# Batched matrix product on one core: x loaded four batches at a time, in place of one batch at a time

## The chip, the cores and the metric

The kernel runs on one core of a Trainium2 chip. The metric is the device time in microseconds (us). A core has five engines that matter here: PE (TensorE, matrix products and transposes), DVE (VectorE) and ACT (ScalarE), which copy and cast, POOL (GpSimd), and SP (SyncE), which only issues transfers. Transfers between HBM (the chip's main memory) and SBUF (the core's working memory, 128 partitions) are carried by 16 DMA engines. PE writes its results to PSUM, from which DVE or ACT copy them to SBUF.

## What is computed

```python
batch, dim_i, dim_j, dim_k = 32, 256, 512, 384
x: (32, 256, 512) float32      y: (32, 512, 384) float32

def reference(x, y):
    return np.einsum('bij,bjk->bik', x, y).astype(np.float32)
```

Each of 32 batches is a product of a 256x512 with a 512x384 matrix. A batch's x is 512 KB, its y 768 KB and its result 384 KB. All of it is read or written once: 16.8 MB, 25.2 MB and 12.6 MB.

## The kernel before

P is 128, NI = 2 (256 rows of i over 128 partitions) and NJ = 4 (512 values of j over 128 partitions). PE contracts over partitions, so x must stand with j on the partitions. HBM has it with i on them, so each batch of x is transposed on PE first.

Five steps are done for each batch b, each by a function of its own:

- `load(b)` (L56) issues two transfers on SP's queue. L61 brings x[b] with two neighbouring rows to each partition: one run of 4 KB per partition. L62 brings y[b] with four neighbouring rows to each partition: one run of 6 KB.
- `transpose(b)` (L64) makes eight 128x128 float32 transposes on PE (L70), two to a PSUM tile of 128x256. DVE (L72) and ACT (L74) copy two such tiles each to `xt_sb` and cast them to float16. The columns of j are taken with a stride of four (`t::NJ`), which fits the four rows of y that stand on one partition.
- `round_y(b)` (L76) casts y[b] to float16 in four pieces of 128x384, two on ACT (L81) and two on DVE (L83).
- `multiply(b)` (L85) makes eight float16 products of 128x128 with 128x384 (L94), which add up in two PSUM tiles.
- `collect(b)` (L103) copies these to `o_sb`, one on ACT (L109) and one on DVE (L111). `store(b)` (L114) issues the result's transfer (L123), one run of 3 KB per partition. It stands on SP's queue, except for batches 27, 29 and 31 (`ON_ACT`), which ACT issues.

The order is written out by hand: `keep` holds every engine to the program's order. Five batches are loaded ahead (`AHEAD`), and then step s of the main loop does `load(s+5)`, `collect(s-2)`, `transpose(s)`, `round_y(s)`, `multiply(s-1)`, `store(s-2)`. In step 31 alone the product of batch 30 stands ahead of the transposes.

Two further things set the order of transfers. SP works its issues off in order, so a store that waits for its results holds up the loads behind it. And the framework gives the transfers eight completion semaphores in turn, so that each issue also waits until the transfer eight places before it has landed. In the program's order of SP, for instance, the 18th issue (a load of x) waits for the semaphore that the 10th used. So at most eight transfers are in flight.

Buffers: seven of x and seven of y, four each of `y_r` and `xt_sb`, eight of `o_sb`, and four PSUM tiles each for the transposes and for the products.

Of the kernel before, what the change touches and what calls it, by code (L numbers as in the profile page):

```python
# [1 line left out]

# [5 lines left out]


MM_DT = mybir.dt.float16  # L10
F32 = mybir.dt.float32
P = 128
AHEAD = 5

ON_ACT = (27, 29, 31)
GROUPS = [1, 1, 1, 1, 1, 1, 1, 1, 1, 1, 1, 1, 1, 1, 1, 1, 1, 1, 1, 1, 1, 1, 1, 1, 1, 1, 1, 1, 1, 1, 1, 1]

@with_exitstack  # L20
def kernel(
    ctx: ExitStack,
    tc: tile.TileContext,
    x: bass.AP,
    y: bass.AP,
    out: bass.AP,
):
    nc = tc.nc

    B, I, J = x.shape  # L30
    _, _, K = y.shape

    NI = I // P
    NJ = J // P

    const_pool = ctx.enter_context(tc.tile_pool(name="const", bufs=1))
    x_pool = ctx.enter_context(tc.tile_pool(name="x_pool", bufs=AHEAD + 2))
    y_pool = ctx.enter_context(tc.tile_pool(name="y_pool", bufs=AHEAD + 2))
    yr_pool = ctx.enter_context(tc.tile_pool(name="yr_pool", bufs=4))
    xt_pool = ctx.enter_context(tc.tile_pool(name="xt_pool", bufs=4))  # L40
    o_pool = ctx.enter_context(tc.tile_pool(name="o_pool", bufs=8))
    tpsum_pool = ctx.enter_context(tc.tile_pool(name="tpsum", bufs=4, space=bass.MemoryType.PSUM))
    opsum_pool = ctx.enter_context(tc.tile_pool(name="opsum", bufs=4, space=bass.MemoryType.PSUM))


    keep = tc.keep_in_program_order

    identity = const_pool.tile([P, P], F32)
    make_identity(nc, identity)


    place = [(g, i, n) for g, n in enumerate(GROUPS) for i in range(n)]
    assert len(place) == B
    x_of, y_of, yr_of, xt_of, ps_of, o_of = {}, {}, {}, {}, {}, {}

    def load(b):  # L56


        x_of[b] = x_pool.tile([P, NI, J], F32, name="x_sb")
        y_of[b] = y_pool.tile([P, NJ, K], F32, name="y_sb")  # L60
        keep(nc.sync.dma_start(out=x_of[b], in_=x[b].rearrange("(p r) j -> p r j", p=P)))  # L61
        keep(nc.sync.dma_start(out=y_of[b], in_=y[b].rearrange("(q t) k -> q t k", q=P)))  # L62

    def transpose(b):  # L64
        x_sb = x_of.pop(b)
        xt_of[b] = xt_pool.tile([P, NJ, NI, P], MM_DT, name="xt_sb")
        for t in range(NJ):
            t_ps = tpsum_pool.tile([P, NI, P], F32, name="t_ps")
            for r in range(NI):
                keep(nc.tensor.transpose(t_ps[:, r], x_sb[:, r, t::NJ], identity))  # L70
            if t % 2 == 0:
                keep(nc.vector.tensor_copy(xt_of[b][:, t], t_ps))  # L72
            else:
                keep(nc.scalar.copy(xt_of[b][:, t], t_ps))  # L74

    def round_y(b):  # L76
        y_sb = y_of.pop(b)
        yr_of[b] = yr_pool.tile([P, NJ, K], MM_DT, name="y_r")
        for t in range(NJ):
            if t % 2 == 0:  # L80
                keep(nc.scalar.copy(yr_of[b][:, t], y_sb[:, t]))  # L81
            else:
                keep(nc.vector.tensor_copy(yr_of[b][:, t], y_sb[:, t]))  # L83

    def multiply(b):  # L85
        xt_sb, y_r = xt_of.pop(b), yr_of.pop(b)
        ps_of[b] = [
            opsum_pool.tile([P, K], F32, name=f"o_ps_{r}", tag="o_ps")
            for r in range(NI)
        ]  # L90
        for t in range(NJ):
            for r in range(NI):
                keep(
                    nc.tensor.matmul(  # L94
                        ps_of[b][r],
                        xt_sb[:, t, r],
                        y_r[:, t],
                        start=(t == 0),
                        stop=(t == NJ - 1),
                    )  # L100
                )

    def collect(b):  # L103
        g, i, n = place[b]
        if i == 0:
            o_of[g] = o_pool.tile([P, n, NI, K], F32, name="o_sb", tag=f"o_sb_{min(n, 2)}")
        for r in range(NI):
            if r % 2 == 0:
                keep(nc.scalar.copy(o_of[g][:, i, r], ps_of[b][r]))  # L109
            else:  # L110
                keep(nc.vector.tensor_copy(o_of[g][:, i, r], ps_of[b][r]))  # L111
        del ps_of[b]

    def store(b):  # L114
        g, i, n = place[b]
        if i < n - 1:
            return
        o_sb = o_of.pop(g)
        dst = out[b - i : b + 1].rearrange("b (p r) k -> p b (r k)", p=P)
        src = o_sb.rearrange("p b r k -> p b (r k)")  # L120
        if n == 1:
            eng = nc.scalar if b in ON_ACT else nc.sync
            keep(eng.dma_start(out=dst[:, 0], in_=src[:, 0]))  # L123

    for b in range(AHEAD):
        load(b)
    for s in range(B + 2):
        if s + AHEAD < B:
            load(s + AHEAD)
        if s >= 2:  # L130
            collect(s - 2)
        if s == B - 1:
            multiply(s - 1)
        if s < B:
            transpose(s)
            round_y(s)
        if 1 <= s != B - 1 and s <= B:
            multiply(s - 1)
        if s >= 2:
            store(s - 2)  # L140


# [1 line left out]
_INS = ['x', 'y']  # L144
_OUTS = [((32, 256, 384), 'float32')]


# [23 lines left out]
```

## Time and profile before

| | |
|---|---|
| device time, median of 3 runs | 137.59 us (137.29 to 137.73) |
| device time of the profiled execution | 137.29 us |
| span of that execution, first to last instruction | 135.5 us |
| granted TensorE clock | 0.993 of full |
| bytes moved | 54.64 MB, 403 GB/s over the span |
| packets (one per run, and one per transfer and DMA engine for its semaphore) | 13833, of them 1536 under 512 B |
| busy: PE, DVE, ACT | 82.2, 64.5 and 66.7 us (61, 48 and 49%) |
| x, y and result: median us from issue to landing (on SP's queue) | 10.2, 11.2, 10.9 |

[...] Busy shares are of the span. "DMA" in the profile is the mean busy share of the 16 DMA engines, and "GB/s" what they moved. The busy share can read a little above 1, because an engine's packets overlap. A mean busy time of one PE instruction includes its overlap with its neighbours.

### The profile page before, as it was taken

To read this page: it belongs to the slowest core of one execution; us is meant where nothing else is said; L and a number is where in the kernel's file an instruction comes from. 1 tells how busy PE (TensorE), PEld (TensorE's weight loads), DVE (VectorE), ACT (ScalarE), POOL (GpSimd) and SP (SyncE) were. 2 spreads that over 40 slices of the span, in tenths; PEclk is the share of its full clock that TensorE was granted. 3 is DMA by queue.
4 is the path that set the end of the run, shared out by engine and by line. 5 is a ranking of instruction groups with operands and counts; after the bars stand their busy time and mean duration, and the time that the engine had idled before them with its cause. 6 is when DMAs were issued, how large, how long until landed. Compare 5 with 4: busy or idle time off the path is not lost.

```text
span 135.5 us, 1734 instructions
## 1 busy us (share of the span) xinstructions
PE 82.2 (61%) x512; PEld 57.4 (42%) x512; DVE 64.5 (48%) x160; ACT 66.7 (49%) x161; POOL 0.7 (1%) x6
## 2 busy tenths in 40 slices
PE   0579778857256775555775555775555775559340
PEld 0466555535233554333554333554333554335310
DVE  0445766656146644546644546644545644545430
ACT  3257766666056644446644446644446644446430
POOL 2000000000000000000000000000000000000000
PEclk9999999999999999999999999999999999999997
DMA  4999999999999999999999999999999999999993
GB/s 154 408 423 420 416 416 416 391 418 418 412 419 412 427 417 420 420 416 418 428 420 418 414 423 421 424 420 418 415 424 420 410 425 421 415 418 419 412 393 130
DMA packets 13833, 54.64 MB, mean 403 GB/s; under 512 B 1536, under 2 KB 1536, under 8 KB 13824
## 3 DMA queue, kind: packets, MB, share of 16 engines
q1 hardware_dynamic: 13392, 53.35, 96.5%
q10 hardware_dynamic: 432, 1.18, 2.2%
q8 instruction: 4, 0.07, 0.2%
q14 instruction: 5, 0.04, 0.1%
HBM read 41.94 MB, written 12.58 MB: 402 GB/s over the span
## 4 chain that ended last, share of the span: by engine, by line
DMA 89%; SPq 2%; PE 2%; issue 1%; DVE 1%; ACT 1%; ACTq 0%
DMA y_sb<-in_y_dram 34%; DMA x_sb<-in_x_dram 30%; DMA out_dram<-o_sb 25%; PE o_ps L94 1%; SPq L61 1%; SPq L62 1%; PE t_ps L70 1%; DVE o_sb L111 1%; ACT y_r L81 0%; ACT o_sb L109 0%; ACTq L123 0%; SPq L123 0%
## 5 line engine op out<-in xcount | busy, mean ns | idle before, releaser
L70 PE MATMUL t_ps<-identity,x_sb 128*128 128x128 f32 x256 | 39.9, 301 | 46.8 <-DMA x_sb<-in_x_dram 44.0
L70 PEld LDWEIGHTS t_ps<-identity,x_sb 128*128 128x128 f32 x256 | 34.4, 211 | 57.6 <-DVE o_sb L111 44.1
L74 ACT CAST xt_sb<-t_ps 128x256 f16<-128x256 f32 x64 | 23.8, 373 | 55.5 <-issue 39.5
L72 DVE CAST xt_sb<-t_ps 128x256 f16<-128x256 f32 x64 | 27.1, 425 | 49.2 <-PE t_ps L70 47.3
L94 PE MATMUL o_ps<-y_r,xt_sb 128*128 128x384 f16 x256 | 47.4, 330 | 1.1 <-ACT y_r L81 1.1
L81 ACT CAST y_r<-y_sb 128x384 f16<-128x384 f32 x64 | 29.6, 510 | 6.2 <-DMA y_sb<-in_y_dram 5.8
L94 PEld LDWEIGHTS <-xt_sb 128*128 128x128 f16 x256 | 25.7, 100 | 14.6 <-issue 1.8
L83 DVE CAST y_r<-y_sb 128x384 f16<-128x384 f32 x64 | 20.1, 356 | 12.4 <-DMA y_sb<-in_y_dram 12.1
L111 DVE COPY o_sb<-o_ps 128x384 f32<-128x384 f32 x32 | 17.8, 558 | 4.6 <-PE o_ps L94 2.1
L109 ACT COPY o_sb<-o_ps 128x384 f32<-128x384 f32 x32 | 15.1, 472 | 1.2 <-PE o_ps L94 1.2
L74 ACT ACT_TABLE_LOAD x1 | 1.3, 1283 | 0.7 <-PEq L155 0.7
masks.py:199 POOL TENSOR_SCALAR_AFFINE_SELECT identity<-identity 128x128 f32<-128x128 f32 x1 | 0.3, 294 | 0.1
masks.py:197 POOL MEMSET identity<- 128x128 f32 x1 | 0.2, 205 | 0.3 <-POOLq L155 0.3
L155 POOL MEMSET const-bfloat16-1.0<- 128x1 bf16 x1 | 0.1, 102 | 0.0
L155 POOL MEMSET const-uint8-127<- 128x1 uint8 x1 | 0.1, 102 | 0.0
L155 POOL MEMSET const-float32-0.0<- 128x1 f32 x1 | 0.1, 99 | 0.2 <-issue 0.2
L155 POOL MEMSET const-float32-1.0<- 128x1 f32 x1 | 0.1, 99 | 0.0
## 6 DMA issues: line engine op xcount, KB each, us to landing
y_sb<-in_y_dram SPq DMA_DIRECT2D x32, 768.0 KB, 11.2
x_sb<-in_x_dram SPq DMA_DIRECT2D x32, 512.0 KB, 10.2
out_dram<-o_sb SPq DMA_DIRECT2D x29, 384.0 KB, 10.9
out_dram<-o_sb ACTq DMA_DIRECT2D x3, 384.0 KB, 4.6
```

The costliest lines, as they stand in the source:

```text
L61: keep(nc.sync.dma_start(out=x_of[b], in_=x[b].rearrange("(p r) j -> p r j", p=P)))
L62: keep(nc.sync.dma_start(out=y_of[b], in_=y[b].rearrange("(q t) k -> q t k", q=P)))
L70: keep(nc.tensor.transpose(t_ps[:, r], x_sb[:, r, t::NJ], identity))
L72: keep(nc.vector.tensor_copy(xt_of[b][:, t], t_ps))
L74: keep(nc.scalar.copy(xt_of[b][:, t], t_ps))
L81: keep(nc.scalar.copy(yr_of[b][:, t], y_sb[:, t]))
L83: keep(nc.vector.tensor_copy(yr_of[b][:, t], y_sb[:, t]))
L94: nc.tensor.matmul(ps_of[b][r], xt_sb[:, t, r], y_r[:, t], start=(t == 0), stop=(t == NJ - 1),)
L109: keep(nc.scalar.copy(o_of[g][:, i, r], ps_of[b][r]))
L111: keep(nc.vector.tensor_copy(o_of[g][:, i, r], ps_of[b][r]))
L155: nc = _bacc.Bacc("TRN2", target_bir_lowering=False, num_devices=1)
```

## The change

x is loaded four batches at a time: a tile of 128 partitions holds batches 4q to 4q+3, 32 partitions to a batch, with eight neighbouring rows of a batch on one partition. The tile is 2 MB, and each partition's part is one run of 16 KB. There are three such tiles. The transfer is issued where the first of the four batches is loaded.

A 128x128 transpose now takes one row position (0 to 7) of all four batches together. For each quarter t of j and each parity e of the row, four transposes fill a PSUM tile of 128x512. One copy for each such tile regroups it by batch as it casts, so that the float16 writes have a stride of four elements. All 32 transposes and eight copies of four batches stand in one step, every fourth. Each `xt_sb` tile holds four batches, and there are two of them.

The look-ahead is six batches in place of five. y has 10 buffers in place of seven, `o_sb` 10 in place of eight. The product of the step before stands ahead of the transposes in all steps. All stores are issued by SP. y's load, its casts, the products, the copies of the results and the bytes of every transfer in total are as before.

```diff
-AHEAD = 5
-ON_ACT = (27, 29, 31)
+Q = 4
+LAG = 8
+ON_ACT = ()
...
+    R = Q * NI
+    PQ = P // Q
...
-    x_pool = ctx.enter_context(tc.tile_pool(name="x_pool", bufs=AHEAD + 2))
-    y_pool = ctx.enter_context(tc.tile_pool(name="y_pool", bufs=AHEAD + 2))
+    x_pool = ctx.enter_context(tc.tile_pool(name="x_pool", bufs=3))
+    y_pool = ctx.enter_context(tc.tile_pool(name="y_pool", bufs=10))
...
-    xt_pool = ctx.enter_context(tc.tile_pool(name="xt_pool", bufs=4))
-    o_pool = ctx.enter_context(tc.tile_pool(name="o_pool", bufs=8))
+    xt_pool = ctx.enter_context(tc.tile_pool(name="xt_pool", bufs=2))
+    o_pool = ctx.enter_context(tc.tile_pool(name="o_pool", bufs=10))
...
     def load(b):
+        if b % Q == 0:
+            x_of[b // Q] = x_pool.tile([P, R, J], F32, name="x_sb")
+            keep(
+                nc.sync.dma_start(
+                    out=x_of[b // Q],
+                    in_=x[b : b + Q].rearrange("g (p r) j -> (g p) r j", r=R),
+                )
+            )
...
-        x_of[b] = x_pool.tile([P, NI, J], F32, name="x_sb")
-        keep(nc.sync.dma_start(out=x_of[b], in_=x[b].rearrange("(p r) j -> p r j", p=P)))
...
-    def transpose(b):
+    def transpose(q):
...
+        xt_of[q] = xt_pool.tile([P, Q, NJ, NI, PQ, Q], MM_DT, name="xt_sb")
+        n = 0
         for t in range(NJ):
-            t_ps = tpsum_pool.tile([P, NI, P], F32, name="t_ps")
-            for r in range(NI):
-                keep(nc.tensor.transpose(t_ps[:, r], x_sb[:, r, t::NJ], identity))
...
+            for e in range(NI):
+                t_ps = tpsum_pool.tile([P, Q, Q, PQ], F32, name="t_ps")
+                for h in range(Q):
+                    keep(
+                        nc.tensor.transpose(
+                            t_ps[:, h].rearrange("c g p -> c (g p)"),
+                            x_sb[:, h * NI + e, t::NJ],
+                            identity,
+                        )
+                    )
+                dst = xt_of[q][:, :, t, e].rearrange("c g p h -> c h g p")
+                if n % 2 == 0:
+                    keep(nc.vector.tensor_copy(dst, t_ps))
+                else:
+                    keep(nc.scalar.copy(dst, t_ps))
+                n += 1
...
     def multiply(b):
-        xt_sb, y_r = xt_of.pop(b), yr_of.pop(b)
+        xt_sb, y_r = xt_of[b // Q][:, b % Q], yr_of.pop(b)
...
-    for b in range(AHEAD):
+    ahead = LAG - 2
+    for b in range(ahead):
         load(b)
     for s in range(B + 2):
-        if s + AHEAD < B:
-            load(s + AHEAD)
+        if s + ahead < B:
+            load(s + ahead)
         if s >= 2:
             collect(s - 2)
-        if s == B - 1:
+        if 1 <= s <= B:
             multiply(s - 1)
+        if s < B and s % Q == 0:
+            transpose(s // Q)
         if s < B:
-            transpose(s)
             round_y(s)
-        if 1 <= s != B - 1 and s <= B:
-            multiply(s - 1)
         if s >= 2:
             store(s - 2)
```

More of the change, by code (lines that the diff above doesn't have):

```diff
@@ L12 @@
 P = 128
-AHEAD = 5
-ON_ACT = (27, 29, 31)
-GROUPS = [1, 1, 1, 1, 1, 1, 1, 1, 1, 1, 1, 1, 1, 1, 1, 1, 1, 1, 1, 1, 1, 1, 1, 1, 1, 1, 1, 1, 1, 1, 1, 1]
+Q = 4
+LAG = 8
+ON_ACT = ()
 @with_exitstack
@@ L49 @@
     make_identity(nc, identity)
-    place = [(g, i, n) for g, n in enumerate(GROUPS) for i in range(n)]
-    assert len(place) == B
     x_of, y_of, yr_of, xt_of, ps_of, o_of = {}, {}, {}, {}, {}, {}
     def load(b):
-        x_of[b] = x_pool.tile([P, NI, J], F32, name="x_sb")
+        if b % Q == 0:
[6 more added lines that the diff above has]
+            )
         y_of[b] = y_pool.tile([P, NJ, K], F32, name="y_sb")
-        keep(nc.sync.dma_start(out=x_of[b], in_=x[b].rearrange("(p r) j -> p r j", p=P)))
         keep(nc.sync.dma_start(out=y_of[b], in_=y[b].rearrange("(q t) k -> q t k", q=P)))
-    def transpose(b):
-        x_sb = x_of.pop(b)
-        xt_of[b] = xt_pool.tile([P, NJ, NI, P], MM_DT, name="xt_sb")
+    def transpose(q):
+        x_sb = x_of.pop(q)
+        xt_of[q] = xt_pool.tile([P, Q, NJ, NI, PQ, Q], MM_DT, name="xt_sb")
+        n = 0
         for t in range(NJ):
-            t_ps = tpsum_pool.tile([P, NI, P], F32, name="t_ps")
-            for r in range(NI):
[L70 to L74, printed above, removed]
+            for e in range(NI):
[14 more added lines that the diff above has]
+                n += 1
     def round_y(b):
@@ L85, in multiply @@
     def multiply(b):
-        xt_sb, y_r = xt_of.pop(b), yr_of.pop(b)
+        xt_sb, y_r = xt_of[b // Q][:, b % Q], yr_of.pop(b)
         ps_of[b] = [
-            opsum_pool.tile([P, K], F32, name=f"o_ps_{r}", tag="o_ps")
-            for r in range(NI)
+            opsum_pool.tile([P, K], F32, name=f"o_ps_{e}", tag="o_ps")
+            for e in range(NI)
         ]
         for t in range(NJ):
-            for r in range(NI):
+            for e in range(NI):
                 keep(
                     nc.tensor.matmul(
-                        ps_of[b][r],
-                        xt_sb[:, t, r],
+                        ps_of[b][e],
+                        xt_sb[:, t, e].rearrange("c p h -> c (p h)"),
                         y_r[:, t],
@@ L103, in collect @@
     def collect(b):
[L104 to L109, printed above, removed]
+        o_of[b] = o_pool.tile([P, NI, K], F32, name="o_sb")
+        for e in range(NI):
+            if e % 2 == 0:
+                keep(nc.scalar.copy(o_of[b][:, e], ps_of[b][e]))
             else:
-                keep(nc.vector.tensor_copy(o_of[g][:, i, r], ps_of[b][r]))
+                keep(nc.vector.tensor_copy(o_of[b][:, e], ps_of[b][e]))
         del ps_of[b]
     def store(b):
[L115 to L123, printed above, removed]
-    for b in range(AHEAD):
+        eng = nc.scalar if b in ON_ACT else nc.sync
+        keep(eng.dma_start(out=out[b].rearrange("(m e) k -> m e k", m=P), in_=o_of.pop(b)))
+    ahead = LAG - 2
+    for b in range(ahead):
         load(b)
     for s in range(B + 2):
-        if s + AHEAD < B:
-            load(s + AHEAD)
+        if s + ahead < B:
+            load(s + ahead)
         if s >= 2:
             collect(s - 2)
-        if s == B - 1:
+        if 1 <= s <= B:
             multiply(s - 1)
+        if s < B and s % Q == 0:
+            transpose(s // Q)
         if s < B:
-            transpose(s)
             round_y(s)
-        if 1 <= s != B - 1 and s <= B:
-            multiply(s - 1)
         if s >= 2:
```

## The prediction

> **What bounds the kernel now.** I read the page's slices first, then its chain of work that ended last.
>
> ```profile
> DMA  4999999999999999999999999999999999999993
> GB/s 154 408 423 420 416 416 416 391 418 418 412 419 412 427 417 420 420 416 418 428 420 418 414 423 421 424 420 418 415 424 420 410 425 421 415 418 419 412 393 130
> ...
> DMA 89%; SPq 2%; PE 2%; issue 1%; DVE 1%; ACT 1%; ACTq 0%
> ```
>
> The 16 DMA engines are full from the second slice to the last but one, and 89% of the chain is transfers. PE, DVE and ACT wait for loads. So the time is the start, the bytes over the rate, and the end. The change leaves the bytes alone (54.5 MB of data). It can act in four ways only: on the rate, on the start, on the end, or by letting the DMA engines run dry in between.
>
> Next, the transfers by stretch: 3 to 15 us (loads only, since the first store is issued at 16.9), 40 to 120 us (the mix) and 128.1 to 129.6 us (stores only, since the last y landed at 128.05).
>
> ```profile
> DMA packets 1088, 4.99 MB, mean 416 GB/s; under 512 B 125, under 2 KB 125, under 8 KB 1088
> ```
> ```profile
> DMA packets 8509, 33.57 MB, mean 420 GB/s; under 512 B 940, under 2 KB 940, under 8 KB 8502
> ```
> ```profile
> DMA packets 229, 0.62 MB, mean 414 GB/s; under 512 B 27, under 2 KB 27, under 8 KB 229
> ```
>
> Data packets (all but those under 512 B) average 5.2, 4.4 and 3.1 KB in these. The rate hardly follows the size.
>
> Last the end, by stretches and in order of time (columns of the first: length, five engines, PE clock, DMA share, GB/s).
>
> ```profile
> 130.00:131.00 1.00, 0.10 (x1) 0.00 (x0) 0.56 (x1) 0.45 (x1) 0.00 (x0) 1.00 1.02 409
> 131.00:132.00 1.00, 0.00 (x0) 0.00 (x0) 0.00 (x0) 0.00 (x0) 0.00 (x0) 1.00 0.85 341
> 132.00:133.00 1.00, 0.00 (x0) 0.00 (x0) 0.00 (x0) 0.00 (x0) 0.00 (x0) 1.00 0.84 335
> 133.00:134.00 1.00, 0.00 (x0) 0.00 (x0) 0.00 (x0) 0.00 (x0) 0.00 (x0) 0.79 0.35 141
> ```
> ```profile
> 128.07 0.51 ACT L81 CAST y_r<-y_sb 128x384 f16<-128x384 f32 x1
> 128.16 0.34 ACTq L123 DMA_DIRECT2D out_dram<-o_sb  x1
> ...
> 130.19 0.56 DVE L111 COPY o_sb<-o_ps 128x384 f32<-128x384 f32 x1 [0.92 <-ACT o_sb L109]
> 130.82 0.34 ACTq L123 DMA_DIRECT2D out_dram<-o_sb  x1
> ```
>
> The last store is issued at 130.82, when little is queued, so the engines are not full from 131 on. Store 29 stands on ACT behind the cast of the last y, so it leaves only at 128.16.
>
> **Part 1, the last stores.** From 131 us on, 0.83 MB moves (341 + 335 + 141 + 15 GB/s, 1 us each), until about 134.05. At 414 GB/s it takes 2.0 us and ends at 133.0. So at most 1.05 us is to be won.
> After the change, SP's program order ends: y31, then stores 23 to 31, nine of them (3.54 MB). With eight transfers in flight at most, stores 23 to 29 can be out when y31 lands, at a time T: store 29 needs store 22, which is ahead of y31, and batch 29's copies, which stand ahead of y31's casts on ACT and DVE. These seven hold 2.75 MB, or 6.6 us at 414. Store 30 follows ACT's two casts and its copy (2 x 0.51 + 0.47 = 1.5 us after T). Store 31 follows at T + 2.8, as now (130.82 - 128.05). So the DMA engines stay full with 3.8 us to spare, and the end is their drain. Some taper comes from engines that finish unevenly, and stays. I take 0.8 us off, with bounds of 0.2 (the taper is mostly unevenness) and 1.05. Moving three stores from ACT to SP adds no issue in all, and nothing but stores stands behind them there.
>
> **Part 2, the packets of x.** A run is a packet now: 12288 data packets are 32 x 3 x 128. Afterwards x has 8 x 128 in place of 32 x 128, so each of 16 engines handles 64 x packets in place of 256: 192 fewer. What one costs beyond its bytes comes from the three rows, as 16 x size / rate. Stores: 16 x 3072 / 414 = 118.7 ns. Mix: 16 x 4437 / 420 = 169.0. Loads: 16 x 5182 / 416 = 199.3. Stores against mix: 36.85 ps a byte, so 5.5 ns a packet. Stores against loads: 38.2 ps, so 1.4 ns. Mix against loads: 40.7 ps, so -11.6 ns (less than nothing). Times 192: 1.06 us won, 0.27 won, or 2.2 lost. x is a load, which speaks for the second, but reading may differ from writing beside the size. I take the middle of the first two, 3.4 ns, or 0.65 us won, and keep 2.2 lost and 1.06 won as bounds. The 24 fewer transfers also save 24 semaphore packets per engine; no row prices these alone, and they are inside the 3.4 ns.
>
> [...]
>
> **Part 3, the start.** By 5 us, 1.18 MB has moved. A full 419 GB/s from the first packet (about 1.86) makes 1.32 MB, or 0.32 us more. The thin spot is at 2.0 to 2.3 us, where the first small x (eight packets an engine, 1.2 us) is done and the next transfers only start. A first transfer of 5 us covers that. I take 0.15, of 0 to 0.3.
>
> PE's first transpose moves from 4.2 us to about 7.7 (1.5 MB more at 420 is 3.6). This is hidden: SP issues eight transfers without a wait (two x, six y, 8.9 MB, 21 us of work), then y6, y7, x2 and y8, and only then store 0. That waits for y3, at about 15 us. Its copies are due at about 16: transposes 7.7 to 13, casts and product to 15, copies 0.6.
>
> **Part 4, the work regrouped.** Four batches still have 32 transposes (L70, 8 in 1.21 us, so 4.8 us) and 32 products (8 in 1.46, so 5.8), or 10.7 us of PE in the 16.3 us that their bytes take (4 x 1.704 MB at 419). Copies of 128x512 are not in this trace.
>
> ```profile
> L72 DVE CAST xt_sb<-t_ps 128x256 f16<-128x256 f32 x64 | 27.1, 425 | 49.2 <-PE t_ps L70 47.3
> L109 ACT COPY o_sb<-o_ps 128x384 f32<-128x384 f32 x32 | 15.1, 472 | 1.2 <-PE o_ps L94 1.2
> L111 DVE COPY o_sb<-o_ps 128x384 f32<-128x384 f32 x32 | 17.8, 558 | 4.6 <-PE o_ps L94 2.1
> ```
>
> DVE's slope (558 - 425 over 128) gives 691 ns for 512 columns; ACT's (472 - 373, L74) 571. Four of each replace eight of each: 2.8 for 3.4 us, and 2.3 for 3.0. If the strided writes cost double, 5.5 and 4.6 us: DVE and ACT still do at most 11 us in 16.3. The burst delays results by some 5 us. Store 4q waits anyway for y of batch 4q+5, 20 us behind y of 4q; its copies need only y of 4q+1, 4 us behind, and the burst. So some 11 us are to spare before SP stalls, and seven transfers (over 10 us) are then still queued. Cost: 0. If this cover went (copies four times as dear), PE, DVE and ACT would set the time, tens of us.
>
> **Sum.** 0.8 + 0.65 + 0.15 = 1.6 us off the profiled execution's 137.29: 135.7. That execution was the fastest of three, 0.3 below the median, so against the median 137.59 I forecast **136.0**.
>
> **The rivals.**
> *A: nothing to win.* The bytes and the full DMA engines stay; the taper is unevenness (0.2) and packets are free (0), the start 0.1: 137.3. For it: rates don't rise with size. Against it: store 31's late issue at 130.82.
> *B: long runs read slower.* Place: x's 64 packets per engine, all through the span. Price: the rows' lower end, 2.2 us lost, less 0.95 from the ends, on the median: 138.8. It decides from -5 ns a packet (0.95 lost). For it: loads, with the largest packets, were slower (416) than the mix. Against it: stores, with the smallest, are slower still.
> *C: packets at the upper end*, 1.06, with the ends at 1.05 and 0.3: 2.4 off, 135.2. For it: store against mix.
>
> **How the numbers follow.** Forecast 0.57, A 0.18, B 0.13, C 0.12. A measurement tells about 0.3% (0.4 us) from no change: faster is below 137.2, slower above 138.0. Forecast and C make 0.69 faster, A 0.18 the same, B 0.13 slower. The likeliest case's own range is 135.4 to 136.9. The full one runs from all upper ends (2.4 off, and 0.3 for the spread between runs, 134.9) to B's 138.8.
>
> **What would show it.** Packets about 10370 (9216 of data, 72 x 16 of semaphores). Middle slices at 422 to 425 GB/s for part 2; 415 or less for B. Part 1: after the last y lands, about 3.5 MB move without a gap, and the taper is under 2 us. Part 3: no thin spot at 2.2 us. Part 4: copies of 128x512 near 691 and 571 ns, and no wait of SP for DVE or ACT in mid-span. It would be wrong if the middle slices show a dip every fourth batch, or x moves at another rate.

## The result, and the profile after

The changed kernel takes 136.24 us (median of 4 runs, 136.18 to 136.52) against 137.62 for the kernel before (137.29 to 137.73, 4 runs). The ratio is 0.9907, 95% interval 0.9886 to 0.9929: 1.3 us faster. Its profiled execution took 136.52 us with a span of 134.7. It was the slowest of its four, while the profiled one before was the fastest, so the two spans (134.7 and 135.5) understate the gain.

The page of the changed kernel, its slices, its queue and its chain:

```profile
PEclk9999999999999985686999599599995999559995
DMA  5999999999999999999999999999999999999992
GB/s 131 399 413 423 447 412 416 416 434 414 404 422 451 425 399 424 421 435 437 400 416 430 438 425 410 421 418 454 407 409 425 433 440 402 421 421 413 412 410 84
DMA packets 10375, 54.62 MB, mean 405 GB/s; under 512 B 1152, under 2 KB 1152, under 8 KB 9344
...
DMA 79%; PE 8%; ACT 5%; DVE 2%; issue 2%; SPq 1%; DVEq 0%
```

The DMA engines are still full from end to end, and the bytes are the same. The first slice moved less than before (131 GB/s against 154). Slices at 434 to 454 come back about every fourth batch, where the 16 KB packets pass (13 to 87 of them start in each of these eight slices, by the packet records), with slices at 399 to 404 between them. The prediction named a dip every fourth batch as a sign of being wrong; but the transfers alone with runs of 16 KB (below) swing as much, from 392 to 457, so this is not the engines running dry. The packet count is as forecast. The chain now names PE and ACT for 13% of the span, but a chain follows only what came last; the runs with free stores below show that the waits of stores for results cost nothing that can be measured.

The stretch from 40 to 120 us, transfers only:

```profile
DMA packets 6419, 33.89 MB, mean 424 GB/s; under 512 B 710, under 2 KB 710, under 8 KB 5774
```

It is 424 GB/s, against 420. The end, by stretches (columns as in the prediction):

```profile
130.00:131.00 1.00, 0.00 (x0) 0.00 (x0) 0.00 (x0) 0.00 (x0) 0.00 (x0) 1.00 1.01 402
131.00:132.00 1.00, 0.00 (x0) 0.00 (x0) 0.00 (x0) 0.00 (x0) 0.00 (x0) 0.74 0.77 307
132.00:133.00 1.00, 0.00 (x0) 0.00 (x0) 0.00 (x0) 0.00 (x0) 0.00 (x0) 0.50 0.29 117
133.00:134.00 1.00, 0.00 (x0) 0.00 (x0) 0.00 (x0) 0.00 (x0) 0.00 (x0) 0.50 0.03 12
```

The taper has not gone. The DMA share falls to 0.77, 0.29 and 0.03, as it fell to 0.85, 0.84 and 0.35 before. It starts at 131 us in both; here it moves less and the last transfer lands at 133.9 us, against 134.6. At 128 us 52.95 MB have moved, against 52.57 before (the total, less what the later stretches show). So the changed kernel was already 0.4 MB, or 0.9 us, ahead when the end began.

The copies from PSUM, on ACT and DVE:

```profile
L94 ACT CAST xt_sb<-t_ps 128x512 f16<-128x512 f32 x32 | 39.8, 1350 | 44.0 <-PE t_ps L84 43.9
L92 DVE CAST xt_sb<-t_ps 128x512 f16<-128x512 f32 x32 | 40.1, 1323 | 40.3 <-PE t_ps L84 40.2
```

They take about twice the forecast 571 and 691 ns. SP felt it (its waits: us in total, times, the longest):

```profile
SPq L135 <- DVE o_sb L130: 11.2, 6, 4.0
```

Of this, 4.0 us is one wait in the first 20 us and 7.2 us come after 112; there is none between.

The trace also holds every packet of the DMA engines with its own duration. Their medians, from the records of the kernels named:

| packet | bytes | median ns | kernel |
|---|---|---|---|
| semaphore | 4 | 9 | both |
| result | 3072 | 121 | both |
| x, one batch | 4096 | 159 | before |
| y | 6144 | 234 | both |
| x, two batches | 8192 | 309 | the kernel with two batches to a tile, below |
| x, four batches | 16384 | 611 | after |

These lie on one line: (611 - 121) / (16384 - 3072) = 36.8 ps a byte, and 121 - 3072 x 0.0368 = 7.9 ns for each packet beside its bytes. By this, 192 packets less per engine are 1.5 us, and 24 semaphore packets of 9 ns another 0.2. But durations overlap: in the same records 88% of the packets of each size have another's start 3 to 4 ns before their end (where at most a fifth would by chance). Less this, a packet costs about 4.4 ns, and the 192 about 0.8 us. So the durations alone leave the gain between 0.8 and 1.5 us; the runs below put the price at 6 to 8 ns a packet. What makes up the difference to 4.4 is not shown.

### The profile page after: what moved, and what is told of

Same layout as the page of the kernel before. It is cut to its first block, busy times and chain, and to the rows that moved or that the text cites. A ratio compares the mean times of both kernels' runs of the same rounds, so it can differ in the third digit from the quotient of the medians.

```text
span 134.7 us, 1539 instructions
## 1 busy us (share of the span) xinstructions
PE 89.5 (66%) x512; PEld 66.6 (49%) x512; DVE 73.7 (55%) x128; ACT 80.1 (59%) x129; POOL 0.7 (1%) x6
## 4 chain that ended last, share of the span: by engine, by line
DMA 79%; PE 8%; ACT 5%; DVE 2%; issue 2%; SPq 1%; DVEq 0%
DMA y_sb<-in_y_dram 30%; DMA x_sb<-in_x_dram 27%; DMA out_dram<-o_sb 21%; PE o_ps L115 4%; PE t_ps L84 4%; ACT xt_sb L94 2%; ACT y_r L102 2%; DVE xt_sb L92 1%; DVE y_r L104 1%; DVE o_sb L130 0%; SPq L69 0%; ACT o_sb L128 0%; SPq L63 0%; DVEq L130 0%
## 5 line engine op out<-in xcount | busy, mean ns | idle before, releaser
L94 ACT CAST xt_sb<-t_ps 128x512 f16<-128x512 f32 x32 | 39.8, 1350 | 44.0 <-PE t_ps L84 43.9
L92 DVE CAST xt_sb<-t_ps 128x512 f16<-128x512 f32 x32 | 40.1, 1323 | 40.3 <-PE t_ps L84 40.2
L84 PE MATMUL t_ps<-identity,x_sb 128*128 128x128 f32 x256 | 43.4, 340 | 24.5 <-DMA x_sb<-in_x_dram 24.3
L115 PE MATMUL o_ps<-y_r,xt_sb 128*128 128x384 f16 x256 | 46.3, 342 | 14.9 <-ACT y_r L102 14.9
L84 PEld LDWEIGHTS t_ps<-identity,x_sb 128*128 128x128 f32 x256 | 41.1, 216 | 27.8 <-issue 26.4
L115 PEld LDWEIGHTS <-xt_sb 128*128 128x128 f16 x256 | 26.2, 102 | 34.2 <-issue 19.9
L102 ACT CAST y_r<-y_sb 128x384 f16<-128x384 f32 x64 | 30.2, 527 | 0.6 <-DMA y_sb<-in_y_dram 0.6
```

Of the source, the lines that this page charges most:

```text
L84: nc.tensor.transpose(t_ps[:, h].rearrange("c g p -> c (g p)"), x_sb[:, h * NI + e, t::NJ], identity,)
L92: keep(nc.vector.tensor_copy(dst, t_ps))
L94: keep(nc.scalar.copy(dst, t_ps))
L115: nc.tensor.matmul(ps_of[b][e], xt_sb[:, t, e].rearrange("c p h -> c (p h)"), y_r[:, t], start=(t == 0), stop=(t == NJ - 1),)
```

## The experiments

All ratios are to the kernel before, run on the same chip beside each kernel, with a 95% interval. The kernels with free stores or with the transfers alone write a constant output; they only show times. Theories: (1) the gain is the longer runs, and the taper is DMA engines that finish unevenly; (2) the gain is as predicted, mostly the last stores; (3) the slow strided copies hold up the last stores.

| kernel | us, median | ratio |
|---|---|---|
| before, all stores on SP | 137.29 | 0.9991 (0.9978 to 1.0004) |
| changed, three stores on ACT | 136.55 | 0.9934 (0.9917 to 0.9952) |
| changed, runs of 4 KB | 137.70 | 1.0019 (1.0006 to 1.0032) |
| changed, regrouped on the read side | 136.31 | 0.9922 (0.9902 to 0.9941) |
| transfers alone, 4 KB | 136.67 | 0.9945 (0.9931 to 0.9959) |
| transfers alone, 16 KB | 135.01 | 0.9824 (0.9807 to 0.9841) |
| first four batches singly | 136.37 | 0.9925 (0.9909 to 0.9941) |
| two batches, 8 KB | 136.66 | 0.9952 (0.9934 to 0.9969) |
| changed, stores free | 136.23 | 0.9911 (0.9895 to 0.9927) |
| before, stores free | 137.15 | 0.9984 (0.9971 to 0.9997) |
| transfers alone, 16 KB, and PE | 136.30 | 0.9922 (0.9909 to 0.9935) |
| transfers alone, 16 KB, and copies | 135.68 | 0.9880 (0.9863 to 0.9897) |

**The last stores, alone.** The kernel before with

```diff
-ON_ACT = (27, 29, 31)
+ON_ACT = ()
```

> The kernel before with one edit: all stores are issued by SP. Theory 1 (the gain is the longer runs; the end's taper is the DMA engines finishing unevenly): the end is as before, 137.2 to 137.9 us. Theory 2 (as predicted: the late stores on ACT leave the DMA engines short at the end, worth 0.8 us): 136.8 us, and the DMA share stays at 1 for about 1 us longer ahead of the taper.

137.29 us; the interval reaches from 0.3 us faster to 0.05 slower. Its end:

```profile
130.00:131.00 1.00, 0.00 (x0) 0.00 (x0) 0.00 (x0) 0.00 (x0) 0.00 (x0) 1.00 1.03 415
131.00:132.00 1.00, 0.00 (x0) 0.00 (x0) 0.00 (x0) 0.00 (x0) 0.00 (x0) 1.00 1.04 418
132.00:133.00 1.00, 0.00 (x0) 0.00 (x0) 0.00 (x0) 0.00 (x0) 0.00 (x0) 1.00 0.63 252
133.00:134.00 1.00, 0.00 (x0) 0.00 (x0) 0.00 (x0) 0.00 (x0) 0.00 (x0) 0.64 0.34 138
```

The engines stay full a microsecond longer, just as theory 2 said, and the end does not come sooner: 133 to 134 us still moves 138 GB/s (141 before). A mean share of 16 engines hides this. What ends the kernel is the engine that is furthest behind, and it was busy throughout in both. The traces show it: a transfer ends with 16 landings on its semaphore (1536 for the 96 transfers of the kernel before), taken here as one for each of the 16 DMA engines. From the last store but one to the last, the median landing moves on by 1.17 us in the kernel before and by 0.93 here, so in the kernel before most engines waited for store 31. But the latest landing moves on by 0.92 and 0.94 us, so the latest engine did not wait. Theory 2 falls.

**The changed kernel with the three stores on ACT again.**

```diff
-ON_ACT = ()
+ON_ACT = (27, 29, 31)
```

> The changed kernel with stores 27, 29 and 31 on ACT as before. Theory 1: no difference to the changed kernel, 136.0 to 136.5 us. Theory 2: 0.8 us of the gain goes, 137.0 us. Theory 3 (the strided copies of 1.3 us delay the last results, so that the end of the changed kernel is late in any case): no more than 0.3 us of difference.

0.9934, which is 0.4 us above the changed kernel (0.9907) and 0.2 above the kernel regrouped on the read side (0.9922, same chip). The intervals overlap in both cases, so neither difference is clear of noise. It speaks for theories 1 and 3, but would not rule out theory 2 by itself.

**Runs of 4 KB, with all else of the change.**

```diff
-                    in_=x[b : b + Q].rearrange("g (p r) j -> (g p) r j", r=R),
+                    in_=x[b : b + Q].rearrange("g (p r) j -> p g r j", p=P),
...
-                            x_sb[:, h * NI + e, t::NJ],
+                            x_sb[:, h, e, t::NJ],
...
-                dst = xt_of[q][:, :, t, e].rearrange("c g p h -> c h g p")
+                dst = xt_of[q][:, :, t, e]
```

> The changed kernel, but the 2 MB transfers of x bring four runs of 4 KB to each partition (two rows of each of four batches), so that the copies from PSUM write without a stride; transfers, their number, their order and all else as in the changed kernel. Theory 1: 256 x packets per engine again instead of 64, 7 to 8 ns each beyond their bytes, so 1.3 us of the gain goes; the start gets its 0.35 us back: 137.0 to 137.3 us, middle rate 420 GB/s. Theory 2 (packets 0.65): 136.7. Theory 3: the copies take about 690 and 570 ns and the last store is issued about 2 us sooner after the last load, which gives back some 0.5 us: 136.4 to 136.7.

1.0019: with its run length gone, the change is slower than the kernel before. Between it and the changed kernel lie 1.0019 - 0.9907 = 0.0112, or 1.5 us (1.3 to the kernel regrouped on the read side, which has the same fast copies). About 0.1 to 0.2 us of this is a slower start (1.61 MB against 1.69 and 1.65, see the end of this experiment), which leaves 1.2 to 1.3 us for 192 packets: 6 to 7 ns each, give or take 2 by the intervals. Its stretch from 40 to 120 us and its copies:

```profile
DMA packets 8271, 33.50 MB, mean 419 GB/s; under 512 B 708, under 2 KB 708, under 8 KB 8266
```
```profile
L94 ACT CAST xt_sb<-t_ps 128x512 f16<-128x512 f32 x32 | 18.7, 585 | 66.5 <-PE t_ps L84 66.5
L92 DVE CAST xt_sb<-t_ps 128x512 f16<-128x512 f32 x32 | 22.1, 692 | 61.7 <-PE t_ps L84 61.7
```

The rate is that of before, and the copies take about the forecast 571 and 691 ns. Theory 1 holds; theory 3's fast copies bring no gain here. The 0.3 us above the kernel before are not the packets: this kernel starts slowly too (1.61 MB moved 5 us after the first packet, by the packet records, against 1.85 before).

**Regrouping on the read side.**

```diff
-                dst = xt_of[q][:, :, t, e].rearrange("c g p h -> c h g p")
+                dst, src = xt_of[q][:, :, t, e], t_ps.rearrange("c h g p -> c g p h")
```

> The changed kernel, but the copy from PSUM walks the PSUM tile with the stride (128 elements of float32 between neighbours) and writes float16 without one. Theory 3 (the write's stride costs the copy its 1.3 us, and the late copies hold up the last stores): copies about 690 and 570 ns, last store issued about 2 us sooner, 135.7 to 136.0 us. Theory 1: copies may be faster, the time stays at 136.1 to 136.4 us, because the taper is unevenness. If the stride costs the same on the read side, copies stay at 1.3 us and nothing moves.

```profile
L92 DVE CAST xt_sb<-t_ps 128x512 f16<-128x512 f32 x32 | 22.1, 692 | 58.4 <-PE t_ps L84 58.4
L94 ACT CAST xt_sb<-t_ps 128x512 f16<-128x512 f32 x32 | 18.7, 585 | 62.4 <-PE t_ps L84 62.4
```

The same regrouping, with the stride on the PSUM side, costs nothing over the plain copies of the kernel with runs of 4 KB (585 and 692 ns); on the float16 write it doubles the copy (1350 and 1323 ns). The time stays at 136.31. So the copies are hidden in both cases, and theory 3 falls.

**The transfers alone**, with each run length. All compute is left out:

```diff
+    o_c = const_pool.tile([P, NI, K], F32, name="o_c")
+    nc.vector.memset(o_c, 0.0)
...
     for s in range(B + 2):
...
+        if s >= 2:
+            keep(nc.sync.dma_start(out=out[s - 2].rearrange("(m e) k -> m e k", m=P), in_=o_c))
```

> The transfers of the kernel before alone: all loads, and all stores from one constant tile and on SP; transposes, casts, products and copies are left out, so that no transfer waits for an engine and the output is constant. If the time is the transfers' alone (theory 1), about 137.0 us, like the kernel before, with the same taper of about 3 us at the end. If the late stores or other waits for compute cost it time (theory 2), at least 0.8 us less, 136.5 or below.

> The transfers of the changed kernel alone, in the same way (x in 16 KB runs, 2 MB a transfer; all compute left out, the output is constant). Theory 1: 1.0 to 1.4 us less than the transfers with 4 KB runs (192 packets of about 8 ns less per engine, less the slower start), so about 135.9, like the changed kernel's 136.2. If the strided copies or the burst of transposes cost the changed kernel time, clearly below it, 135.5 or less.

136.67 and 135.01: the transfers alone gain 0.0121 x 137.3 = 1.7 us, a little more than the kernel did. Not all of it is the packets: in the trace with 4 KB one DMA engine lands 0.6 to 0.7 us behind the next from 102 us on, where an instruction packet of 8 KB passes. But each lies below its kernel, by the ratios 0.8 and 1.1 us, so with compute there is something more. Where it shows, for 16 KB (columns: length, DVE, POOL, PE clock, DMA share, GB/s):

```profile
130.00:131.00 1.00, 0.00 (x0) 0.00 (x0) 1.00 1.04 418
131.00:132.00 1.00, 0.00 (x0) 0.00 (x0) 1.00 0.58 234
132.00:133.00 1.00, 0.00 (x0) 0.00 (x0) 1.00 0.03 8
```

The last transfer lands at 132.4 us, 1.5 us sooner than in the changed kernel. Here, without compute, the engines finish nearly together: its 16 landings lie within 0.8 us, against 2.1 us in the changed kernel.

**The first four batches one at a time**, on the kernel with the regrouping on the read side.

```diff
     def load(b):
-        if b % Q == 0:
+        if b < Q:
+            if b == 0:
+                x_of[0] = x_pool.tile([P, R, J], F32, name="x_sb")
+            keep(
+                nc.sync.dma_start(
+                    out=x_of[0][:, b * NI : (b + 1) * NI],
+                    in_=x[b].rearrange("(p r) j -> p r j", p=P),
+                )
+            )
+        elif b % Q == 0:
...
+                if q == 0:
+                    dst = dst.rearrange("c g p h -> c g (p h)")
+                    src = t_ps.rearrange("c h g p -> c h (g p)")
```

> The kernel with the regrouping on the read side, whose first four batches of x come one at a time with runs of 4 KB, as before the change, and the others four at a time. Theory 1: the start's loss (about 0.16 MB by 5 us, 0.35 us) is the first transfer's and goes away, against 24 more packets per engine (0.2 us): 136.0 to 136.2 us, and 1.8 MB or more moved by 5 us after the first packet. If the start's loss has another cause, 136.4 to 136.6.

1.85 MB had moved 5 us after the first packet (1.65 in its parent kernel), so the start's loss belongs to the first transfer. Yet the time did not follow: 136.37 against 136.31. The 24 packets more explain 0.2 us of the 0.35 to 0.5 expected; the rest stays open, within the interval.

**Two batches to a tile.**

```diff
-Q = 4
+Q = 2
...
-    x_pool = ctx.enter_context(tc.tile_pool(name="x_pool", bufs=3))
+    x_pool = ctx.enter_context(tc.tile_pool(name="x_pool", bufs=6))
...
-    xt_pool = ctx.enter_context(tc.tile_pool(name="xt_pool", bufs=2))
+    xt_pool = ctx.enter_context(tc.tile_pool(name="xt_pool", bufs=4))
```

> The changed kernel with two batches to a tile in place of four: runs of 8 KB, transfers of 1 MB, 16 transposes in a burst, twice the tiles of half the size. Theory 1 (a fixed cost per packet of about 8 ns): 128 of the 192 packets are saved, so two thirds of the 1.4 us that lay between the runs of 4 KB and the changed kernel: 136.7 us, and packets of 8 KB at a median of 310 ns. If only the longest runs gain (a matter of 16 KB reads), 137.3 or more.

136.66, and 309 ns a packet, as theory 1 said. From 4 to 8 KB (128 packets) the ratio falls by 0.0067, or 0.9 us: 7 ns a packet. From 8 to 16 KB (64 packets) it falls by 0.0030 to 0.0045, 0.4 to 0.6 us: 6 to 10 ns. So the gain goes with the number of packets, and not with the longest runs alone.

**Free stores, with all compute.** Every store takes its bytes from a constant tile, so none waits for a result.

```diff
-        keep(eng.dma_start(out=out[b].rearrange("(m e) k -> m e k", m=P), in_=o_of.pop(b)))
+        keep(eng.dma_start(out=out[b].rearrange("(m e) k -> m e k", m=P), in_=o_c))
```

> The changed kernel with all its compute, but every store takes its bytes from one constant tile, so that no store waits for a result (the output is constant). It stands between the transfers alone (135.0 us) and the changed kernel (136.2 to 136.3). If the difference of 1.2 to 1.3 us between those is the stores' waits for late results (theory 3), 135.0 to 135.3 us, with the short taper of the transfers alone. If it is something that the compute brings beside the waits, such as the transfers that fetch instructions on single DMA engines (theory 1: unevenness), 136.0 us or more, with the long taper.

> The kernel before with all its compute, all stores on SP and from one constant tile, so that no store waits for a result (the output is constant). It stands between its transfers alone (136.7 us) and the kernel before (137.3). If the late stores cost the 0.6 us, 136.7 us; if the compute brings it beside the waits, 137.2 us.

136.23 and 137.15. SP's 11 us of waits for DVE cost the changed kernel nothing that can be measured. In the kernel before, freeing the stores is worth 0.2 us (0.04 to 0.4); the stores on SP gave 0.1 of it, though that is within noise. What remains between these and the transfers alone (1.2 and 0.5 us) comes with compute, but not through the stores' waits for results.

**What compute brings.** The transfers alone with 16 KB runs, once beside PE work and once beside copies. All other compute is left out.

```diff
+        for n in range(16 if s < B else 0):
+            if n % 4 == 0:
+                t_ps = tpsum_pool.tile([P, Q, P], F32, name="t_ps")
+            keep(nc.tensor.transpose(t_ps[:, n % 4], identity, identity))
```

> The transfers alone with runs of 16 KB, beside 512 transposes of the constant identity on PE, which read nothing that is loaded and hold up no transfer (all other compute is left out, the output is constant). The traces with compute show four transfers of 16 KB on queue q8, of about 1 us each, that the transfers alone do not have; they fetch instructions. If they put single DMA engines behind and so make the long taper (theory 1), these come back and the time goes from 135.0 to about 136.0 us. If it is the copies of DVE and ACT, or the data's own waits, 135.0 to 135.2 us.

```diff
+        for n in range(4 if s < B else 0):
+            a = yr_pool.tile([P, NI, K], MM_DT, name="a")
+            keep(nc.vector.tensor_copy(a, o_c))
+            c = xt_pool.tile([P, NI, K], MM_DT, name="c")
+            keep(nc.scalar.copy(c, o_c))
```

> The transfers alone with runs of 16 KB, beside 128 copies of a constant tile (768 columns) on DVE and 128 on ACT, which read nothing that is loaded and hold up no transfer (all other compute is left out, the output is constant). If the copies' reads and writes of SBUF slow the DMA engines, 135.5 to 136.2 us, with longer packets. If the instruction fetches for PE make the taper (theory 1), 135.0 to 135.2 us.

With PE, 136.30: all of the 1.2 us, from PE work that no transfer waits for. Its queues, PE's slices and its end (columns: length, PE, PE's weight loads, DVE, POOL, PE clock, DMA share, GB/s):

```profile
q1 hardware_dynamic: 10368, 54.53, 98.0%
q8 instruction: 4, 0.07, 0.2%
```
```profile
PE   5999999999999999980000000000000000000000
```
```profile
131.00:132.00 1.00, 0.00 (x0) 0.00 (x0) 0.00 (x0) 0.00 (x0) 0.50 0.64 255
132.00:133.00 1.00, 0.00 (x0) 0.00 (x0) 0.00 (x0) 0.00 (x0) 0.50 0.22 89
133.00:134.00 1.00, 0.00 (x0) 0.00 (x0) 0.00 (x0) 0.00 (x0) 0.50 0.05 17
```

Four transfers of 16 KB on q8, whose kind the profile gives as instruction, are back (0.9 to 1.1 us each by the packet records; fetches, from here on), and so is the long taper. They pass at 16.7, 30.1, 44.0 and 57.8 us. PE was done at 60.2 us, so the taper at 131 to 134 us is nothing that PE did then.

The records do not name the DMA engine of a packet, but the 16 landings of each transfer show how far the engines are apart. Before the first fetch the latest landing is at most 0.6 us behind the median. After the first fetch one landing is 1.8 us behind, after the second two are more than 1 us behind, after the third three and after the fourth four, and these four are still 1.1, 1.4, 1.6 and 1.8 us behind in the last transfer. So with each fetch one more engine came to be more than 1 us behind, and none had caught up by the end. The last transfer's landings in the profiled executions (us from the start of the span):

| kernel | mean of the 16 | last | first to last |
|---|---|---|---|
| before | 133.60 | 134.6 | 1.65 |
| before, all stores on SP | 133.38 | 134.6 | 2.07 |
| changed | 132.48 | 133.9 | 2.12 |
| transfers alone, 4 KB | 133.06 | 134.1 | 1.36 |
| transfers alone, 16 KB | 131.97 | 132.4 | 0.79 |
| the same, and PE | 132.27 | 133.7 | 2.10 |
| the same, and copies | 132.07 | 132.8 | 1.25 |

The mean shows the gain of the longer runs: 1.1 us in the kernel and 1.1 us in the transfers alone, the slower start included. The last landing shows the lag: beside PE work it comes 1.3 us later, while the mean moves by only 0.3. The furthest engine alone sets the end, so the costs of the four fetches, 0.9 to 1.1 us each, did not add up: the last landing moved by 1.3 us.

With copies, 135.68: 0.8 us above (by the ratios) the transfers alone, which neither theory gave. The packets' medians are as they were (121, 234 and 611 ns). Two more instruction packets of 8 KB stand in its records, at 24 and 37 us, and from each on one more landing stays 0.6 to 0.9 us behind the median. The last landing comes 0.4 us later than in the transfers alone, which is the whole difference between these two profiled executions (135.48 and 135.04 us). The rest of the 0.8 us, and whether the copies do anything beside, stays open: no run parts them from their instruction packets.

## Why the prediction was right, and where not

The time (136.0 against 136.24) and the sign came out, and the sum was right while three of its terms were not. That it came out is in good part luck: about 0.7 us too much in part 1 and up to 0.5 too much in part 3 stood against some 0.5 to 0.9 too little in part 2.

- **What bounds it**: held. The transfers alone come within 0.8 and 1.1 us of the two kernels.
- **Part 1, 0.8 us won: wrong.** The step that failed is "At 414 GB/s it takes 2.0 us and ends at 133.0", which took the taper for missing work. Moving the stores alone gave 0.1 us (at most 0.3). The stores did come sooner and the engines did stay full longer; the engine furthest behind ended when it had before. My own reservation, that the taper comes from uneven engines, was the fact, and the trace of before had it: seven of the 16 landings of its last store come 0.8 to 1.5 us behind the median.
- **Part 2, 0.65 us won: right in kind, mis-sized.** By the runs a packet costs 6 to 8 ns beside its bytes and not 3.4, and the longer runs are worth 1.2 to 1.5 us. The upper bound of 5.5 ns was too low: it came from differences of three rates 1% apart, one over a stretch of 1.5 us. The durations of single packets in the trace of before (121, 159 and 234 ns) already lay on the line. At 16 KB no loss showed: 611 ns for 16 KB is 26.8 GB/s per engine, against 25.8 at 4 KB.
- **Part 3, 0.15 us won: wrong in sign.** The thin spot at 2 us grew (82 GB/s from 2 to 3 us, against 295 before). The first 14 packets of 16 KB take 1.0 to 2.1 us each (the median of all is 0.61), and 0.16 MB less had moved 5 us after the first packet (1.69 against 1.85, by the packet records). What that costs at the end is not settled.
- **Part 4, cost 0: right**, with copies at the "double" that it allowed for: DVE and ACT do 73.7 and 80.1 us in 134.7. The 3.8 us to spare at the end were gone (the last store went out at 129.6 us), and this cost nothing that can be measured (136.23 us with free stores), since the lagging engine still had work: the latest landing moved on by 0.94 us from the last store but one to the last.
- **Rivals.** A was right on the taper and wrong on the packets. B (long runs read slower) is ruled out by the packets' line and by the kernel with runs of 4 KB. C was nearest in part 2 and wrong in the ends.

## What to carry to other kernels

In a kernel that the DMA engines bound, price a packet from the durations of single packets in the trace, by size, before reading it from rates; take off what neighbours overlap, and check the price with a run that changes only the run length. Here each run cost 6 to 8 ns beside its bytes, and runs four times as long on 31% of the bytes gave 1%. A mean DMA share below 1 at the end is no proof that a transfer was issued late: here some engines were 0.8 to 1.5 us behind, and issuing the last stores sooner gave no more than 0.3 us. The 16 landings of the last transfers, taken as one for each engine, tell the two apart. When a copy regroups its elements, try the stride on the side of PSUM: here the copies of 512 columns took 692 and 585 ns with it there, against 1323 and 1350 with it on the float16 write.

## What the hardware showed unexpectedly

- Instructions cost transfer time: 512 transposes that touch nothing else took the transfers from 135.0 to 136.3 us. With each of their four fetches one more landing came to be more than 1 us behind the median, and at the end four were 1.1 to 1.8 us behind.
- A float16 write with a stride of four elements (8 bytes) took 1323 ns on DVE and 1350 on ACT for 512 columns, where the same columns without a stride took 692 and 585. With a stride of two (the kernel with two batches) 256 columns took 451 and 452 ns, against 425 and 373 without.
- PE's granted clock fell to half for 3.4 to 6.8 us at a time, six times in the changed kernel before its end. In one of these (stretches, columns as in the prediction), PE waits for a tile of x from 80.5 us, starts again at 83 and is then granted half speed until about 87:

```profile
80.00:81.00 1.00, 0.51 (x4) 0.10 (x1) 0.00 (x0) 0.00 (x0) 0.00 (x0) 1.00 0.82 344
...
82.00:83.00 1.00, 0.00 (x0) 0.00 (x0) 0.00 (x0) 0.00 (x0) 0.00 (x0) 1.00 0.97 397
83.00:84.00 1.00, 0.83 (x6) 0.86 (x7) 0.00 (x0) 0.00 (x0) 0.00 (x0) 0.84 1.03 424
84.00:85.00 1.00, 1.00 (x6) 1.00 (x5) 0.99 (x1) 0.14 (x1) 0.00 (x0) 0.50 1.02 424
...
86.00:87.00 1.00, 1.00 (x7) 1.00 (x6) 1.00 (x1) 0.60 (x2) 0.00 (x0) 0.50 1.06 436
87.00:88.00 1.00, 1.00 (x10) 1.00 (x9) 0.68 (x2) 1.00 (x2) 0.00 (x0) 0.95 0.97 402
```

The mean is 0.887 against 0.993. What brings the fall is not shown. No run prices this here; with free stores the time was the same (136.23 us), so PE's results were not what the end waited for.
